# Ring slots between the heads of the first mixer, and the place of the convolutions in the first two parts of each feed-forward

## Chip, cores and metric

The kernel runs on one core of a Trainium2 chip. The metric is the device time of one execution, in microseconds (us). The core has five engines with queues of their own: TensorE (PE in the profile; its weight loads are PEld), VectorE (DVE), ScalarE (ACT), GpSimd (POOL) and SyncE (SP), which here only issues loads and stores. They wait for each other through semaphores. Before the change three runs took 1823.7, 1823.83 and 1827.47 us, with a median of 1823.83.

## What is computed

A two-layer encoder for 256 prompt tokens and 512 sample tokens of width 1024. Each layer has a mixer and a feed-forward, both with adaptive norms (adaln: shifts, scales and gates that are computed from a condition). The mixer of layer 0 is a two-way mLSTM with four heads; that of layer 1 is windowed attention. All is float32. The parts that the change touches, cut to their core:

```python
# mLSTM, per head and direction
s = einsum('bhtd,bhsd->bhts', qc, kc) * exp(log_d - m_t[..., None])
num = einsum('bhts,bhse->bhte', s, vc) + ...
h = num / maximum(abs(den), exp(-m_t)[..., None])
...
hs = h_fwd + h_bwd
hs = hs * rsqrt(mean(hs * hs, axis=-1, keepdims=True) + EPS) * head_g
out = (hs * sigmoid(o)) @ w_out
...
# feed-forward of width 2816: a convolution of width 3 along the tokens behind the first product
u = conv(h @ w_up)          # two halves, a and b
out = (silu(a) * b) @ w_down
```

## The kernel before

**Products.** A float32 product is made of three products of a narrower format: each operand is split into a high and a low part, and high x high, high x low and low x high are summed in PSUM. The split of a weight is a copy on ScalarE (L272, `whi`) and a subtraction on VectorE (L273, `wlo`); `fp_copy_split` does both. So each 128x1024 block of weights costs one load on SP's queue (`raw`, L281, five buffers), one ScalarE and one VectorE instruction, and then runs on TensorE.

**Slabs.** Large intermediate tensors (q, k and v of a head, the broadcast maxima, the transposed result, the rows of the feed-forward) come from one ring of six slots (`slab`). A slot is given in the order of the requests, and a tensor waits for all readers of the tensor that had the slot before. `hsT`, two slabs that take the transposed results of heads 0 and 1 and of heads 2 and 3, is requested ahead of the loop over the heads, but each is first written when a head closes.

**Order.** A list scheduler fixes the order of instructions on each engine from the program, from the estimated ends of what they wait for, and from explicit constraints (`issue_after`: not before that instruction). On the chip each engine then runs its queue strictly in that order.

**The heads.** The loop over four heads: request `mb` (the slab of this head's maxima, and later of its result), load the two rows of maxima, broadcast to 128 partitions (`maxima`, L751; head 0 loads them later, in `values`), compute q and k (`gemmT` and `keep`, evacuated by L275 and L276), scores with the decays (`E`, from L813 to L823), v, and scores times v for each block of 128 tokens (L866 to L874), with the sums of squares for the norm in `ss` (L878, L879). `close` scales a finished sequence on ScalarE (L732), transposes it on TensorE (L736), and writes it to `hsT` (L740); the close of one head is called inside the next. The adaln products of later norms (`ps<-raw,silc`) fill gaps.

**The feed-forward.** The width of 2816 is cut into eleven parts. `up(p)` computes two pairs of 128-column chunks: i = 0 is the half a, i = 1 the half b. For p of 1 and more `pair` uses a scheme with seven products per pair instead of eight; GpSimd prepares sums of the weights (L1381 to L1393), ScalarE copies a PSUM bank to another twice (L1397 and L1408, the `fork`), so that a sum already made can go on in two ways, and VectorE adds at the end (L1421, L1422). Part 0 is computed by a function of its own, with an order written by hand. Then `conv` runs for each chunk: one ScalarE instruction (L1585) and two on VectorE (L1587, L1588), the outer taps. `silu` (L1595) is on ScalarE, which has to load another function table first; `product` (L1600) multiplies on GpSimd and splits the result `g`, which `down(p)` multiplies by the weights of the second product. What is in the list `held` is run inside the next `pair`, behind its second copy. Before the change `held` holds the silu of the first half for p of 1 and more, and for part 0 the silu and product, which so come in the first pair of part 1.

## Time and profile before

| | |
|---|---|
| median of three runs | 1823.83 us |
| profiled execution | 1823.31 us |
| its span | 1821.4 us |
| VectorE, L273 of weights | 231 times, 1378 ns each, 318.2 us |
| GpSimd, L1600 | 44 times, 1966 ns each, 86.4 us |
| loads of 512 KB of `in_w_dram` | 208, 3.7 us from issue to landing |
| loads of 512 KB of `in_adaln_w_dram` by SP into `raw` | 84, 4.5 us from issue to landing |

The program has two layers one after the other, and in each a mixer and then a feed-forward: the passage from head 0 to head 1 lies between about 115 and 190 us, the first feed-forward starts at about 530 us, the second at about 1300 us. A row of a timeline gives the start in us, the duration, the engine, the line and operation, the tensors out<-in, the shapes, how many such instructions were put together, and in brackets the idle time of the engine before it and what ended that. A row of waits gives engine, tensor and line, what it waited for, then the us in total, the number of waits and the longest. Matmuls are pipelined: the time from one start to the next is the pace, and the duration in a row is longer.

### The profile page before, as it was taken

What the parts mean: (1) busy time and instruction counts of PE and PEld (TensorE: products, weight loads), DVE (VectorE), ACT (ScalarE), POOL (GpSimd) and SP (SyncE); (2) the same over time, 40 slices, a digit from 0 to 9 for tenths busy, and PEclk for the clock granted to TensorE, in tenths of its full rate; (3) what the DMA queues carried; (4) which work ended last, traced back from release to release, by engine and by line L of the source; (5) the groups of instructions that cost most, each with busy time, mean ns of one, the idle gap of its engine ahead of it and who ended that gap; (6) DMA issues with size and microseconds to landing.
All of it is one profiled execution on the core that took longest, in us unless ns stands there. A gap on an engine that the chain in (4) does not pass through costs nothing.

```text
span 1821.4 us, 28979 instructions
## 1 busy us (share of the span) xinstructions
PE 1785.9 (98%) x11290; PEld 1652.4 (91%) x11290; DVE 1390.6 (76%) x2148; ACT 891.4 (49%) x1798; POOL 474.1 (26%) x384
## 2 busy tenths in 40 slices
PE   7999999999999999999999999999999999999998
PEld 4987888889998999999999999889989999999997
DVE  4875677786799777787877867767998777787776
ACT  3553433444455444444444556665564444444443
POOL 2100000031024333333331313330144333333321
PEclk9999999999999999999999999999999999999998
DMA  8334456556212222222222331134122222222212
GB/s 337 122 121 139 158 196 221 190 159 222 95 55 73 69 70 69 64 66 70 70 70 86 113 93 42 56 94 138 47 81 70 70 70 70 70 71 70 70 36 70
DMA packets 64245, 184.48 MB, mean 101 GB/s; under 512 B 6167, under 2 KB 23831, under 8 KB 64108
## 3 DMA queue, kind: packets, MB, share of 16 engines
q1 hardware_dynamic: 63532, 182.11, 31.0%
q8 instruction: 89, 1.46, 0.3%
q10 hardware_dynamic: 576, 0.52, 0.1%
q14 instruction: 48, 0.39, 0.1%
HBM read 176.17 MB, written 6.43 MB: 100 GB/s over the span
## 4 chain that ended last, share of the span: by engine, by line
PE 87%; DVE 5%; ACT 3%; DMA 3%; issue 1%; POOL 1%; SPq 0%; POOLq 0%; DVEq 0%; ACTq 0%
PE ps L266 28%; PE pa L266 24%; PE ps L1348 10%; PE ps L1351 10%; PE ps L1349 10%; DMA raw<-in_w_dram 1%; PE pa L1187 1%; DMA raw<-in_adaln_w_dram 1%; DVE wlo L273 1%; ACT whi L272 1%; DMA slab<-in_adaln_w_dram 0%; PE pa L1349 0%; PE pa L1348 0%; DVE wlo L1473 0%; DVE ada L528 0%
## 5 line engine op out<-in xcount | busy, mean ns | idle before, releaser
L273 DVE TENSOR_TENSOR wlo<-raw,whi 128x1024 fp32r<-128x1024 f32 x231 | 318.2, 1378 | 113.0 <-ACT whi L272 111.1
L272 ACT CAST whi<-raw 128x1024 fp32r<-128x1024 f32 x231 | 241.9, 1049 | 331.9 <-PE pa L266 142.5
L266 PE MATMUL pa<-slab,whi 128*128 128x256 f32 (+1 forms) x1328 | 317.8, 334 | 0.0
L266 PEld LDWEIGHTS pa<-slab,whi 128*128 128x128 f32 x1328 | 230.1, 189 | 21.5 <-DVE slab L606 0.2
L606 DVE SCALAR_TENSOR_TENSOR slab<-pa,mod,slab 128x256 f32<-128x256 f32 (+1 forms) x332 | 192.7, 598 | 63.1 <-PE pa L266 63.0
L266 PE MATMUL pa<-slab,wlo 128*128 128x256 f32 (+1 forms) x664 | 213.0, 333 | 0.0
L266 PE MATMUL ps<-zh,whi 128*128 128x256 f32 (+1 forms) x560 | 187.9, 337 | 0.3 <-ACT zh L946 0.3
L266 PE MATMUL ps<-zl,whi 128*128 128x256 f32 (+1 forms) x560 | 184.1, 331 | 0.5 <-DVE zl L574 0.5
L266 PE MATMUL ps<-zh,wlo 128*128 128x256 f32 (+1 forms) x560 | 180.9, 329 | 0.0
L1348 PE MATMUL ps<-zh,whi 128*128 128x384 f32 x504 | 172.5, 342 | 3.8 <-ACT nt L1419 1.9
L1349 PE MATMUL ps<-zl,whi 128*128 128x384 f32 x504 | 170.1, 337 | 0.8 <-DVE zl L1305 0.8
L1351 PE MATMUL ps<-zh,wlo 128*128 128x384 f32 x504 | 169.2, 336 | 0.0
L266 PE MATMUL ps<-slab,whi 128*128 128x384 f32 (+2 forms) x656 | 163.7, 333 | 0.9 <-DVE slab L273 0.5
L266 PEld LDWEIGHTS pa<-slab,wlo 128*128 128x128 f32 x664 | 125.2, 189 | 13.2 <-DVE wlo L273 0.4
L1384 POOL TENSOR_TENSOR raw<-raw,raw 128x512 f32<-128x512 f32 x40 | 53.8, 1346 | 318.6 <-DVE wlo L273 245.7
L1600 POOL TENSOR_TENSOR slab<-slab 128x772 f32<-128x772 f32 x44 | 86.4, 1966 | 171.1 <-DVE slab L1588 159.2
L1587 DVE SCALAR_TENSOR_TENSOR slab<-slab,cstt,slab 128x771 f32<-128x771 f32 x88 | 108.4, 1233 | 26.6 <-ACT slab L1585 26.4
L528 DVE SCALAR_TENSOR_TENSOR ada<-raw,silc,ada 128x1024 f32<-128x1024 f32 x84 | 109.5, 1333 | 12.8 <-DMA raw<-in_adaln_w_dram 12.8
L266 PEld LDWEIGHTS ps<-zl,whi 128*128 128x128 f32 x560 | 106.3, 190 | 13.3 <-issue 4.2
L266 PEld LDWEIGHTS ps<-zh,whi 128*128 128x128 f32 x560 | 106.4, 190 | 13.2 <-issue 4.3
L266 PEld LDWEIGHTS ps<-slab,whi 128*128 128x128 f32 x656 | 115.3, 188 | 3.4 <-ACT whi L272 0.9
L266 PEld LDWEIGHTS ps<-zh,wlo 128*128 128x128 f32 x560 | 105.2, 190 | 9.1
(304 smaller groups left out, 4302.8 us busy)
## 6 DMA issues: line engine op xcount, KB each, us to landing
raw<-in_w_dram SPq DMA_DIRECT2D x208, 512.0 KB, 3.7
raw<-in_adaln_w_dram SPq DMA_DIRECT2D x84, 512.0 KB, 4.5
slab<-in_x_dram SPq DMA_DIRECT2D x12, 512.0 KB, 7.5
slab<-in_adaln_w_dram SPq DMA_DIRECT2D x12, 512.0 KB, 10.3
slab<-mrows SPq DMA_DIRECT2D x8, 384.0 KB, 4.6
xs<-slab SPq DMA_DIRECT2D x6, 512.0 KB, 3.8
bt<-brow SPq DMA_DIRECT2D x16, 192.0 KB, 3.1
slab<-xs SPq DMA_DIRECT2D x6, 512.0 KB, 7.2
```

Source lines behind the costliest of these rows:

```text
L266: self.nc.tensor.matmul(out, lhsT, rhs, start=start, stop=stop)
L272: nc.scalar.copy(hi, src)
L273: return nc.vector.tensor_tensor(lo, src, hi.bitcast(F32), ALU.subtract)
L528: stt(acc[:, s], row, w, acc[:, s], ALU.mult, ALU.add)
L606: self.nc.vector.scalar_tensor_tensor(x, o, self.mod[l][:, gc + c, q : q + 1], x, ALU.mult, ALU.add)
L1187: nc.tensor.transpose(pp[:, ks], b.t[:, e, ks], self.ident)
L1348: mm(o, wh[:, k], hi[k], start=start and k == 0, stop=False, skip_group_check=True)
L1349: mm(o, wh[:, k], lo[k], start=False, stop=False, skip_group_check=True)
L1351: mm(o, wl[:, k], hi[k], start=False, stop=k == 3, skip_group_check=True)
L1384: tt(q[0], q[2], q[0], ALU.subtract)
L1587: stt(y[:, 1:], u[:, :-1], w(0), y[:, 1:], ALU.mult, ALU.add)
L1600: nc.gpsimd.tensor_tensor(y, y, yrow[:, j], ALU.mult)
```

## The change

Two parts, in one diff.

In the mLSTM, `maxima` becomes a function of the head and its slab. The slab of the next head's maxima (`soon`) is requested and loaded in the body of the head before, ahead of the loop over the tokens, and at heads 0 and 2 a GpSimd memset writes one column of the `hsT` slab that this and the next head fill. Both move the moment at which a slot of the ring is taken.

In the feed-forward, `taps(urow, yrow, p, i)` names the two convolutions of a half. Part 0 runs those of its half a at once; those of its half b go to the first pair of part 1 behind its second copy, and its silu and product to the second pair, at the same place. Part 1 runs its convolutions, silu and product after both of its pairs. From part 2 on nothing changes, but the constraint on held work now names the low half of a weight split (`wb_low`) too.

```diff
     def split(self, src):
...
-        self.fp_copy_split(hi, lo, src)
+        self.low = self.fp_copy_split(hi, lo, src)
         return hi, lo
...
+        def maxima(h, mb):
+            for d in range(2):
+                r = d * 32 + h
+                nc.sync.dma_start(mb[:, d], md[r : r + 1, :].to_broadcast([P, T]))
...
         for h in range(4):
 
-            mb = self.slab([P, 4, T])
-
-            def maxima():
...
-            if h:
-                maxima()
+            if h == 0:
+                mb = self.slab([P, 4, T])
+            else:
+                mb = soon
...
+            if h < 3:
+                soon = self.slab([P, 4, T])
+                maxima(h + 1, soon)
+            if h % 2 == 0:
+                nc.gpsimd.memset(hsT[h // 2][:, 0, 0:1], 0.0)
             ss = pool.tile([P, T6], F32, tag="ss", name=self.nm("ss"), bufs=2)
...
         wb = self.split(rb)
+        wb_low = self.low
...
         if behind:
-            with self.tc.issue_after(fork.ins):
+            with self.tc.issue_after(fork.ins), self.tc.issue_after(wb_low.ins):
                 behind()
...
+        def taps(urow, yrow, p, i):
+            for j in range(2):
+                conv(urow[:, 2 * i + j], yrow[:, 2 * i + j], i * FC + 2 * p + j)
...
-                for j in range(2):
-                    conv(urow[:, 2 * i + j], yrow[:, 2 * i + j], i * FC + 2 * p + j)
-                if i == 0:
-                    held.append(lambda: silu(yrow))
-            if p:
-                product(yrow, g)
-            else:
-                gate = held.pop()
-                held.append(lambda: (gate(), product(yrow, g)))
+                if p > 1:
+                    taps(urow, yrow, p, i)
+                    if i == 0:
+                        held.append(lambda: silu(yrow))
+            if p == 0:
+                taps(urow, yrow, 0, 0)
+                held.extend((lambda: (silu(yrow), product(yrow, g)), lambda: taps(urow, yrow, 0, 1)))
+                return g
+            if p == 1:
+                for i in range(2):
+                    taps(urow, yrow, 1, i)
+                silu(yrow)
+            product(yrow, g)
             return g
```

The order of SP's queue around the maxima of heads 0, 1 and 2 (slab_677, slab_1300 and slab_2168 are their slabs), before:

```order
L715 DMA mrows<-slab_294 36x768
L751 DMA slab_677<-mrows 128x768 x2
L281 DMA raw_1462<-in_adaln_w_dram 128x1024
L281 DMA raw_1464<-in_adaln_w_dram 128x1024
L281 DMA raw_1467<-in_w_dram 128x1024
L281 DMA raw_1500<-in_adaln_w_dram 128x1024
L281 DMA raw_1531<-in_w_dram 128x1024
L281 DMA raw_1564<-in_adaln_w_dram 128x1024
L281 DMA raw_1595<-in_adaln_w_dram 128x1024
L751 DMA slab_1300<-mrows 128x768 x2
L751 DMA slab_2168<-mrows 128x768 x2
L281 DMA raw_1625<-in_adaln_w_dram 128x1024
```

And with the change (slab_677, slab_1135 and slab_1965):

```order
L715 DMA mrows<-slab_294 36x768
L732 DMA slab_677<-mrows 128x768 x2
L732 DMA slab_1135<-mrows 128x768 x2
L281 DMA raw_1463<-in_adaln_w_dram 128x1024
L281 DMA raw_1465<-in_adaln_w_dram 128x1024
L281 DMA raw_1468<-in_w_dram 128x1024
L281 DMA raw_1501<-in_adaln_w_dram 128x1024
L281 DMA raw_1532<-in_w_dram 128x1024
L281 DMA raw_1565<-in_adaln_w_dram 128x1024
L281 DMA raw_1596<-in_adaln_w_dram 128x1024
L732 DMA slab_1965<-mrows 128x768 x2
L281 DMA raw_1626<-in_adaln_w_dram 128x1024
```

Head 1's maxima moved ahead of seven weight loads, right behind head 0's; head 2's stayed where they were.

VectorE at the close of head 0, where the low half of head 1's q (slab_1303) is written from four PSUM tiles (L276), before:

```order
L740 TENSOR_SCALAR slab_675<-pa_1286,cstt 128x512
L872 TENSOR_SCALAR slab_677<-pa_1271,dn_1262,slab_677 128x256
L740 TENSOR_SCALAR slab_675<-pa_1292,cstt 128x512
L276 TENSOR_SCALAR slab_1303<-ps_1310,slab_1303 128x512
L276 TENSOR_SCALAR slab_1303<-ps_1351,slab_1303 128x256
L276 TENSOR_SCALAR slab_1303<-ps_1388,slab_1303 128x512
L276 TENSOR_SCALAR slab_1303<-ps_1419,slab_1303 128x256
L878 TENSOR_SCALAR ss_1135<-ss_1135 128x2
```

With the change the first two of the four stand far ahead of the close (which writes slab_675 in L745, 36 rows below the last row shown here), among the scores of head 0:

```order
L273 TENSOR_TENSOR PT_1060<-E_1051,PT_1059 128x640
L276 TENSOR_SCALAR slab_1304<-ps_1311,slab_1304 128x512
L724 COPY eT<-pa_1127 128x216
L813 TENSOR_SCALAR E_1088<-slab_677,aT,kct 128x128
L273 TENSOR_TENSOR PT_1078<-E_1070,PT_1077 128x640
L813 TENSOR_SCALAR E_1088<-slab_677,aT,kct 128x128
L813 TENSOR_SCALAR E_1110<-slab_677,aT,kct 128x128 x2
L273 TENSOR_TENSOR wlo_1535<-raw_1532,whi_1534 128x1024
L276 TENSOR_SCALAR slab_1304<-ps_1352,slab_1304 128x256
```

The block of four behind the first writes of `hsT` is taken apart.

ScalarE in the first feed-forward, around the silu of part 0 (slab_5576; L1408 is the second copy of the first pair of part 1), before:

```order
L1585 ACTIVATE slab_5576<-slab_5126,cstt 128x772
L1408 COPY ps_4555<-ps_4554 128x384
L1595 ACT_TABLE_LOAD
L1595 ACTIVATE slab_5576<-slab_5576 128x772
L272 COPY whi_5708<-raw_5698 128x1024
L1361 COPY slab_5126<-pa_5398 128x128
L1361 COPY slab_5126<-pa_5398 128x256
L272 COPY slab_5577<-slab_5576 128x772
L1585 ACTIVATE slab_5576<-slab_5126,cstt 128x772
L1595 ACTIVATE slab_5576<-slab_5576 128x772
```

And with the change (L1414 is now the second copy, here of the second pair; L1601 the silu; slab_5578 part 0; slab_5579 its product, slab_5586 part 1):

```order
L1414 COPY ps_4557<-ps_4556 128x384
L1601 ACT_TABLE_LOAD
L1601 ACTIVATE slab_5578<-slab_5578 128x772 x2
L272 COPY s1h_6082<-raw_6071 128x512
L1425 COPY nt_5753<-ps_4557 128x384
L1408 COPY nt_5982<-ps_4555 128x384
L272 COPY slab_5579<-slab_5578 128x772
L1591 ACTIVATE slab_5586<-slab_5129,cstt 128x772 x2
L272 COPY whi_5875<-raw_5873 128x1024
L272 COPY slab_5579<-slab_5578 128x772
L1591 ACTIVATE slab_5586<-slab_5129,cstt 128x772
```

The table load, the silu and the casts of part 0's product moved from the first pair of part 1 to behind the second copy of the second; part 1's convolutions (L1591) stand between the two casts.

More of the change, by code (lines that the diff above doesn't have):

```diff
@@ L744, in mlstm @@
         for h in range(4):
-            mb = self.slab([P, 4, T])
-            def maxima():
-                for d in range(2):
-                    r = d * 32 + h
-                    nc.sync.dma_start(mb[:, d], md[r : r + 1, :].to_broadcast([P, T]))
-            if h:
-                maxima()
+            if h == 0:
+                mb = self.slab([P, 4, T])
+            else:
+                mb = soon
             qk = []
@@ L786, in evac @@
                         self.step(self.fillp)
-                self.gemmN(U_MIN + 3 * h + 2, evac, None if h else (decay, maxima))
+                self.gemmN(U_MIN + 3 * h + 2, evac, None if h else (decay, lambda: maxima(0, mb)))
                 return v
```

## The prediction

> **What bounds the kernel now.** I read the page's busy shares first, then the waits of TensorE by stretch, then the order of time around the places where TensorE stands still.

> ```profile
> span 1821.4 us, 28979 instructions
> ...
> PE 1785.9 (98%) x11290; PEld 1652.4 (91%) x11290; DVE 1390.6 (76%) x2148; ACT 891.4 (49%) x1798; POOL 474.1 (26%) x384
> ```

> TensorE is busy for 1785.9 of 1821.4 us, so no edit can win more than 35.5 us by removing idle time, plus what a low clock costs inside busy time. The profiled execution took 1823.31 us, 1.9 more than its span, and the median of the runs is 1823.83, 0.5 above it. The waits of TensorE from 125 to 190 us (heads 0 and 1 of the first layer) come first, those from 540 to 580 us (the start of the first feed-forward) second; from 1305 to 1350 us (the second feed-forward) the three largest rows read the same.

> ```profile
> PE ps L266 <- DVE slab L276: 2.4, 1, 2.4
> PE pa L266 <- ACT slab L272: 1.5, 1, 1.5
> PE pa L736 <- ACT slab L732: 0.8, 1, 0.8
> ```

> ```profile
> PE ps L1351 <- DVE s1l L273: 1.4, 1, 1.4
> PE ps L1348 <- ACT nt L1419: 1.0, 1, 1.0
> PE ps L1348 <- ACT ps L1397: 0.7, 1, 0.7
> ```

> These two places are the ones that the change edits. The windows (TensorE, weight load, VectorE, ScalarE, GpSimd busy, then the granted clock) show what else happens there.

> ```profile
> 140.00:145.00 5.00, 5.00 (x34) 2.52 (x27) 2.09 (x8) 1.88 (x5) 0.72 (x1) 0.50 0.00 0
> ```

> ```profile
> 560.00:565.00 5.00, 3.63 (x21) 3.26 (x20) 5.00 (x5) 4.28 (x8) 3.37 (x2) 1.00 0.34 105
> ```

> After the stall in the heads the clock is granted at 0.50; in the feed-forward it stays at 1.00, and VectorE is busy without a break.

> **The heads: ring slots in order of need.** The rows of TensorE, with those of the engines that it waits for:

> ```profile
> 135.76 1.63 PE L736 MATMUL pa<-kct,slab 128*128 128x128 f32 x8 [0.75 <-ACT slab L732]
> 139.77 3.63 PE L266 MATMUL ps<-raw,silc 128*32 128x256 f32 x30 [2.38 <-DVE slab L276]
> 143.33 0.80 PE L266 MATMUL ps<-zh,whi 128*128 128x512 f32 x1
> ...
> 145.47 0.39 PE L266 MATMUL ps<-zh,wlo 128*128 128x512 f32 x1
> 145.70 0.40 PE L266 MATMUL ps<-zh,whi 128*128 128x512 f32 x1
> ...
> 146.86 0.38 PE L736 MATMUL pa<-kct,slab 128*128 128x128 f32 x2
> 146.99 0.48 PE L266 MATMUL ps<-zh,wlo 128*128 128x512 f32 x1
> ```

> ```profile
> 181.51 1.07 PE L266 MATMUL ps<-raw,silc 128*32 128x256 f32 x16
> 184.08 0.51 PE L266 MATMUL pa<-slab,PT 128*128 128x258 f32 x2 [1.50 <-ACT slab L272]
> ```

> ```profile
> 137.32 0.75 DVE L740 TENSOR_SCALAR slab<-pa,cstt 128x512 f32<-128x512 f32 x1 [1.61 <-PE pa L736]
> ...
> 139.03 1.94 DVE L276 SCALAR_TENSOR_TENSOR slab<-ps,slab 128x512 fp32r<-128x512 f32 x4
> ```

> ```profile
> 182.42 1.04 ACT L272 CAST whi<-raw 128x1024 fp32r<-128x1024 f32 x1 [1.62 <-DMA raw<-in_w_dram]
> ...
> 183.67 0.35 ACT L272 CAST slab<-ps 128x256 fp32r<-128x256 f32 x1
> ```

> The evacuations of head 1's q (L275, L276) run as one block of four behind head 0's close (L740), because q's slot comes after that of hsT in the ring. Their four PSUM tiles stay full until 139.03 and later, and the adaln matmuls have no bank. In the changed order the same eight instructions stand one by one between the score and value work of head 0, each behind the product that it evacuates, and the transposes of L736 stand between the products of head 1's k. So these stalls go:
> - the wait of 0.75 ahead of the transposes;
> - their pace: eight take 1.63, while a pair later takes 0.13 (146.86 to 146.99), four pairs 0.5: 1.1;
> - the wait of 2.38 for a bank;
> - the low clock after it. Thirty adaln matmuls take 3.56 us (139.77 to 143.33) where sixteen at full clock take 1.07, thirty then 2.0: 1.6. The five products from 143.33 to 145.47 take 2.14 where one a 0.23 (145.47 to 145.70) makes 1.15: 1.0. Together 2.6;
> - the wait of 1.50 at 184: the copy of v (183.67) stands behind a weight copy that waits for its load (182.42). In the new order two more v products (48 matmuls of 128x256) stand between that v product and its reader; at half of 0.23 each these are 5.5 us of cover for 1.5.

> Sum: 0.75 + 1.1 + 2.4 + 2.6 + 1.5 = 8.3 us. What is added: one GpSimd memset of 128x1 at heads 0 and 2, on an engine that is 26% busy; and the two loads of head 1's maxima, moved ahead of three weight loads.

> ```profile
> 127.20 21.59 SPq L751 DMA_DIRECT2D slab<-mrows  x4
> ```

> ```profile
> SPq L751 <- PE pa L736: 19.6, 1, 19.6
> ```

> ```profile
> slab<-mrows SPq DMA_DIRECT2D x8, 384.0 KB, 4.6
> ```

> The four maxima loads hold SP for 21.59 us, of which 19.6 wait for the last transposes of head 0; two adaln loads and head 1's v weights are queued behind. The change takes only two of the four out; head 2's still wait for the close at the same place. So the block ends no later than before, by as much earlier as the close is, and the v weights have the cover that they had. The two moved loads (4.6 us to landing) delay weights that are read only some 30 us later. I put both at zero. The bounds of this part: 4.2 if the waits go but a stall elsewhere still takes the clock down and the wait at 184 stays (0.75 + 1.1 + 2.4), 8.3 if nothing comes instead. All four heads are ordered anew, and TensorE hardly waits in the other three, so a little can only be lost there; I take 7.5.

> [...]

> **The feed-forward: work behind the copies.** Both layers have the same new order. VectorE's work stays the same; only its place changes. Prices:

> ```profile
> 547.57 1.28 ACT L1595 ACT_TABLE_LOAD   x1
> 548.86 0.85 ACT L1595 ACTIVATE slab<-slab 128x772 f32<-128x772 f32 x1
> ...
> 552.33 0.84 ACT L272 CAST slab<-slab 128x772 fp32r<-128x772 f32 x1 [1.24 <-POOL slab L1600]
> 553.07 1.03 ACT L1585 ACTIVATE slab<-slab,cstt 128x772 f32<-128x772 f32 x1
> ...
> 558.73 0.48 ACT L1397 COPY ps<-slab 128x384 f32<-128x384 f32 x1 [2.59 <-DVE slab L1421]
> ```

> ```profile
> 547.82 1.21 DVE L273 TENSOR_TENSOR wlo<-raw,whi 128x1024 fp32r<-128x1024 f32 x1
> ...
> 561.15 2.14 DVE L273 TENSOR_TENSOR s1l<-raw,s1h 128x512 fp32r<-128x512 f32 x1
> ...
> 566.38 1.01 DVE L1588 SCALAR_TENSOR_TENSOR slab<-slab,cstt,slab 128x771 f32<-128x771 f32 x1
> 567.31 0.95 DVE L273 TENSOR_TENSOR slab<-slab,slab 128x772 fp32r<-128x772 f32 x1
> ```

> ```profile
> 549.79 2.51 POOL L1600 TENSOR_TENSOR slab<-slab 128x772 f32<-128x772 f32 x1 [5.97 <-ACT slab L1595]
> ...
> 560.90 1.84 POOL L1600 TENSOR_TENSOR slab<-slab 128x772 f32<-128x772 f32 x1 [4.43 <-DVE slab L1588]
> ```

> ```profile
> 561.63 0.34 PE L1349 MATMUL ps<-zl,s1h 128*128 128x384 f32 x1
> 563.35 0.44 PE L1351 MATMUL ps<-zh,s1l 128*128 128x384 f32 x1 [1.37 <-DVE s1l L273]
> ```

> Removed: the three waits, 1.4 + 1.0 + 0.7 = 3.1; and each costs a little more than its row says: 561.63 to 563.35 is 1.72, and the pace of 128x384 is 0.17 (three quarters of the 0.23), so the third costs 1.55 where its row has 1.37. With the same 0.17 on each, 3.6 a layer. s1l and the copies no longer stand behind part 0's silu and product.

> Added: the silu and products of part 0 come behind the second copy of pair two, and down(0), which needs them, directly behind that pair. Three waits can take the place:
> - the first pair's sums (L1422) still stand behind the taps: 0 to 1.0, I take 0.3.
> - the second copy of pair two now has no product between its input and its reader. TensorE waits for the copy, 0.48, and its signals: 0.7.
> - down(0). From the end of that copy TensorE has three products of twelve, 36 x 0.17 = 6.2 us. Table load 1.28, silu 0.85, GpSimd 1.84 to 2.51, cast 0.84: the first high half is there after 4.8 to 5.5, in time; its low half, 0.95 more, too. The second half is later: ScalarE puts two conv starts of part 1 (2 x 1.03) and a weight copy (1.04) ahead of its cast, ready at 8.7 to 9.4. VectorE, idle before, then has three taps, a weight low half, a tap and the product's low half: 4 x 1.01 + 1.21 + 0.95 = 6.2 from about 6.4, ready at 12.6 (12 to 13.5). TensorE has used up its 6.2 and twelve products of 0.23, then four more, by 9.9, waits 0.9 for a weight copy, and stands again from 11.2: 1.4, bounds 0.8 to 2.3. Small waits behind it 0.3. In all 2.6, bounds 1.9 to 3.5.

> Sum 0.3 + 0.7 + 2.6 = 3.6, bounds 2.6 to 5.2: nothing gained or lost against the 3.6 removed, from -1.0 to +1.6 a layer. I take 0 for both layers, bounds -2.0 to +3.2.

> Forecast: 1823.3 - 7.5 + 0 = 1815.8 by the profiled execution, 0.5 more by the median: **1816**.

> **Rivals.**
> 1. The heads' gain is partly given back. For: SP still waits 19.6 us for the close; head 1's v weights now sit behind reads of the adaln weights that come a little later. A load (4.6 as that of the maxima), copy 1.04 and low half 1.21 make 6.9, against 24 score products of 0.23, 12 half as wide and nine thin adaln ones, 7 to 8 us. If that cover fails and the clock falls again, only the 4.2 stay: 1819.6, or half a us more.
> 2. The feed-forward gains in full. For: VectorE has the same work with fewer clashes with GpSimd (s1l at 2.14). Against: the chain above. Without new waits 2 x 3.6 more: 1809.
> 3. Slower: the clock. If the stand ahead of down(0) reaches the 2.4 us that brought 0.50 at 140, each layer pays 2.6 for the clock besides the upper bound of its waits: (5.2 - 3.6 + 2.6) x 2 = 8.4, more than the 7.5 of the heads; with the heads at their 4.2 it ends at 1823.8 - 4.2 + 8.4 = 1828. It decides from a stand of 2.4 us; mine is 1.4. Against: 560 to 565 holds stands of 1.4 at clock 1.00.
> 4. The change does not do it: the slots still come late. The new order speaks against it; 1823.8.

> **How the numbers follow.** Forecast 0.62, rival 1 0.14, rival 2 0.10, rival 3 0.11, rival 4 0.03. A change under 0.2%, 3.6 us, can't be told from none: faster is below 1820.2. The forecast and rival 2 lie there, and of rival 1 about a third: 0.77. Rival 4 and the rest of rival 1: 0.12. Rival 3: 0.11. The likeliest case's own range is 1813 to 1819.5 (8.3 and -2.0 to 7.5 and +3.2); the range of 1809 to 1824 takes in the first two rivals and leaves out the third.

> **What would show it.** Right: no wait of L276 and no window of clock under 0.9 between 125 and 190, TensorE busy there for all but about 1 us; behind the second copy of pair two (near 555 in a span that is shorter) a wait of 0.7 and, at down(0), one or two of 1 to 2 us on L273. Wrong: a new TensorE wait over 1 us between 125 and 400, a clock of 0.5 in the feed-forward, or a feed-forward that loses less than 2 or more than 5 us a layer.

## The result, and the profile after

The changed kernel is slightly slower: its median is 1827.14 us (1824.25 to 1831.24, nine runs) where the kernel before has 1823.73 (1823.44 to 1827.47, nine runs). The ratio is 1.0020, with a 95% interval of 1.0011 to 1.0029. The forecast was 1816 within 1809 to 1824, so both the size and the direction were wrong. The profiled execution took 1831.24 us, the longest of the nine; before's took 1823.31.

The top of the page of the changed kernel, span and busy time of each engine:

```profile
span 1829.4 us, 28977 instructions
...
PE 1791.7 (98%) x11290; PEld 1654.3 (90%) x11290; DVE 1383.3 (76%) x2148; ACT 889.5 (49%) x1798; POOL 474.6 (26%) x386
```

TensorE has the same 11290 instructions as before and is busy for 5.8 us longer, so the first question is where the clock fell. These are windows of the changed kernel (busy time of TensorE, weight load, VectorE, ScalarE, GpSimd, then the granted clock): the place of the old stall in the heads first, then the start of down(0) in both layers.

```profile
140.00:145.00 5.00, 5.00 (x35) 4.46 (x34) 1.43 (x7) 2.13 (x8) 0.69 (x1) 1.00 0.01 2
...
575.00:580.00 5.00, 3.87 (x10) 3.10 (x11) 5.00 (x7) 1.00 (x2) 1.73 (x1) 0.66 0.33 105
1360.00:1365.00 5.00, 3.19 (x8) 2.58 (x9) 5.00 (x6) 1.67 (x2) 1.05 (x1) 0.66 0.36 105
```

The last two stretches before:

```profile
575.00:580.00 5.00, 5.00 (x34) 4.72 (x33) 5.00 (x6) 2.52 (x4) 1.52 (x2) 1.00 0.34 105
1360.00:1365.00 5.00, 5.00 (x34) 4.81 (x33) 5.00 (x7) 1.59 (x3) 4.63 (x3) 1.00 0.08 34
```

The clock of 0.50 between the heads is gone, as forecast; a new low clock stands in each feed-forward, where it was 1.00. The waits of TensorE in the feed-forward of the first layer (540 to 600 us) show what comes ahead of it:

```profile
PE pa L266 <- DVE slab L273: 2.4, 1, 2.4
PE ps L1353 <- ACT ps L1414: 0.6, 1, 0.6
PE ps L1353 <- DVE slab L1428: 0.4, 1, 0.4
```

The three waits of before (1.4, 1.0, 0.7) are gone. Of those that came instead, 0.37 for the sums and 0.61 for the second copy are what the prediction had (0.3 and 0.7), but the stand ahead of down(0) is 2.40 where 1.4 was forecast. TensorE's rows there:

```profile
573.39 0.34 PE L1354 MATMUL ps<-yl,whi 128*128 128x384 f32 x1
576.13 0.65 PE L266 MATMUL pa<-slab,whi 128*128 128x512 f32 x1 [2.40 <-DVE slab L273]
576.58 0.63 PE L266 MATMUL pa<-slab,wlo 128*128 128x512 f32 x1
...
579.14 0.63 PE L266 MATMUL pa<-slab,wlo 128*128 128x512 f32 x1
579.57 0.42 PE L1356 MATMUL ps<-yh,wlo 128*128 128x384 f32 x1
```

Eight products take 3.44 us (576.13 to 579.57), 0.43 each. VectorE's rows show what the product of part 0 was waiting behind (L1593 and L1594 are the sums of the convolutions; the two `slab<-slab,slab` of L273 are the low halves of the product):

```profile
559.59 1.23 DVE L273 TENSOR_TENSOR wlo<-raw,whi 128x1024 fp32r<-128x1024 f32 x1 [0.40 <-ACT whi L272]
566.12 1.21 DVE L273 TENSOR_TENSOR s1l<-raw,s1h 128x512 fp32r<-128x512 f32 x1 [5.30 <-ACT s1h L272]
567.25 0.54 DVE L1428 TENSOR_TENSOR slab<-pa,nt 128x384 f32<-128x384 f32 x1
567.72 2.15 DVE L273 TENSOR_TENSOR slab<-slab,slab 128x772 fp32r<-128x772 f32 x1
569.80 0.55 DVE L1427 TENSOR_TENSOR slab<-ps,nt 128x384 f32<-128x384 f32 x1
570.26 1.94 DVE L1593 SCALAR_TENSOR_TENSOR slab<-slab,cstt,slab 128x771 f32<-128x771 f32 x2
...
574.19 1.01 DVE L1594 SCALAR_TENSOR_TENSOR slab<-slab,cstt,slab 128x771 f32<-128x771 f32 x1
575.12 0.95 DVE L273 TENSOR_TENSOR slab<-slab,slab 128x772 fp32r<-128x772 f32 x1
```

VectorE, which worked here without a break before, stands idle for 5.30 us at 560.8 to 566.1; then the sums of part 1 come ahead of the product's second low half, which TensorE needs and which ends at 576.07.

In the heads the picture is the other way round. The waits of TensorE from 100 to 400 us:

```profile
PE ps L266 <- DMA raw<-in_adaln_w_dram: 1.7, 1, 1.7
PE pa L266 <- DVE E L823: 1.2, 2, 0.7
PE ps L266 <- ACT whi L272: 0.6, 1, 0.6
PE ps L266 <- DVE wlo L273: 0.6, 2, 0.3
PE ps L491 <- DVE sb L487: 0.4, 1, 0.4
```

None of the three waits of before (2.4, 1.5, 0.8) is left, and SP still stands 19.2 us for head 2's maxima, both as forecast. But there are five new rows. To see their effect I match each TensorE instruction with the same one of the profile before and take the median difference of the starts, the *shift*. It is -5.4 at 150 to 160 and still -5.1 at 200 to 230, then -3.7 at 270 to 290, -1.7 at 310 to 340 and 0.0 from 350 on. The heads win about 5 us and have lost them again 120 us later. The first feed-forward adds 2.5; the second takes the shift from 2.8 to 6.2. Of these 3.4, 0.9 comes ahead of the first pair, with a wait of 0.84 for `zl` that stands with 0.94 to 0.96 in e1, e8 and e10 below too, two of which have the old feed-forward; the other 2.5 are those of the first layer again. The span grows by 8.0; the last 1.6 of it come behind 1800 us, and e4 below, whose shift is 0.0 up to there, has 1.7 there too.

### The profile page after: what moved, and what is told of

Its sections match the earlier page's. It is cut to its first block, busy times and chain, and to the rows that moved or that the text cites. A ratio compares the mean times of both kernels' runs of the same rounds, so it can differ in the third digit from the quotient of the medians.

```text
span 1829.4 us, 28977 instructions
## 1 busy us (share of the span) xinstructions
PE 1791.7 (98%) x11290; PEld 1654.3 (90%) x11290; DVE 1383.3 (76%) x2148; ACT 889.5 (49%) x1798; POOL 474.6 (26%) x386
## 4 chain that ended last, share of the span: by engine, by line
PE 82%; DVE 7%; DMA 4%; ACT 4%; issue 2%; POOL 0%; SPq 0%; POOLq 0%; DVEq 0%; ACTq 0%
PE ps L266 24%; PE pa L266 23%; PE ps L1353 11%; PE ps L1356 10%; PE ps L1354 10%; DMA raw<-in_w_dram 2%; DMA raw<-in_adaln_w_dram 2%; PE pa L1192 1%; ACT whi L272 1%; DVE ada L528 1%; DVE wlo L273 1%; PE pa L1354 1%; PE pa L1353 1%; PE pa L1356 1%; DMA slab<-in_adaln_w_dram 0%
## 5 line engine op out<-in xcount | busy, mean ns | idle before, releaser
L272 ACT CAST whi<-raw 128x1024 fp32r<-128x1024 f32 x231 | 241.8, 1049 | 361.1 <-PE pa L266 154.8
L273 DVE TENSOR_TENSOR wlo<-raw,whi 128x1024 fp32r<-128x1024 f32 x231 | 309.0, 1339 | 115.8 <-ACT whi L272 113.8
L266 PE MATMUL pa<-slab,whi 128*128 128x256 f32 (+1 forms) x1328 | 319.6, 335 | 4.8 <-DVE slab L273 4.8
L266 PEld LDWEIGHTS pa<-slab,whi 128*128 128x128 f32 x1328 | 231.3, 189 | 27.6 <-DVE slab L273 5.8
L606 DVE SCALAR_TENSOR_TENSOR slab<-pa,mod,slab 128x256 f32<-128x256 f32 (+1 forms) x332 | 193.2, 598 | 72.1 <-PE pa L266 72.0
L266 PE MATMUL pa<-slab,wlo 128*128 128x256 f32 (+1 forms) x664 | 214.3, 335 | 0.0
L266 PE MATMUL ps<-zh,whi 128*128 128x256 f32 (+1 forms) x560 | 187.6, 336 | 0.9 <-ACT whi L272 0.6
L266 PE MATMUL ps<-zl,whi 128*128 128x256 f32 (+1 forms) x560 | 183.4, 330 | 0.5 <-DVE zl L574 0.5
L266 PE MATMUL ps<-zh,wlo 128*128 128x256 f32 (+1 forms) x560 | 180.5, 328 | 0.6 <-DVE wlo L273 0.6
L266 PE MATMUL ps<-slab,whi 128*128 128x384 f32 (+2 forms) x656 | 163.7, 332 | 0.9 <-DVE slab L273 0.5
L266 PEld LDWEIGHTS pa<-slab,wlo 128*128 128x128 f32 x664 | 126.3, 190 | 13.1
L1593 DVE SCALAR_TENSOR_TENSOR slab<-slab,cstt,slab 128x771 f32<-128x771 f32 x88 | 112.2, 1279 | 25.7 <-ACT slab L1591 25.6
L266 PEld LDWEIGHTS ps<-zh,whi 128*128 128x128 f32 x560 | 106.1, 190 | 13.9 <-issue 3.9
L266 PEld LDWEIGHTS ps<-slab,whi 128*128 128x128 f32 x656 | 115.2, 188 | 3.4 <-ACT whi L272 0.9
L266 PEld LDWEIGHTS ps<-zl,whi 128*128 128x128 f32 x560 | 106.0, 190 | 12.2 <-issue 3.4
L266 PEld LDWEIGHTS ps<-zh,wlo 128*128 128x128 f32 x560 | 104.9, 189 | 10.1 <-DVE wlo L273 1.0
## 6 DMA issues: line engine op xcount, KB each, us to landing
slab<-mrows SPq DMA_DIRECT2D x8, 384.0 KB, 4.7
```

What stands on the lines that cost most here:

```text
L266: self.nc.tensor.matmul(out, lhsT, rhs, start=start, stop=stop)
L272: nc.scalar.copy(hi, src)
L273: return nc.vector.tensor_tensor(lo, src, hi.bitcast(F32), ALU.subtract)
L606: self.nc.vector.scalar_tensor_tensor(x, o, self.mod[l][:, gc + c, q : q + 1], x, ALU.mult, ALU.add)
L1593: stt(y[:, 1:], u[:, :-1], w(0), y[:, 1:], ALU.mult, ALU.add)
```

## The experiments

Two theories were tried. The first: the heads' half of the change is worth nothing in the end, since its gain is given back by new waits in heads 2 and 3, and the feed-forward half is the whole loss, by the stand ahead of down(0) and its clock. The rival: heads 2 and 3 are limited by the stream of weights anyhow, and the rest is spread between runs. That spread is large enough to matter: over the later runs the kernel before had medians of 1824.46 to 1825.94 with single runs between 1820.1 and 1831.5. Each kernel is compared below with the runs of before beside it, and shifts are against the one profile of before.

| kernel | what it holds of the change | median us | before beside it | ratio, 95% interval |
|---|---|---|---|---|
| e1_heads | heads half | 1823.79 | 1824.81 | 0.9996 (0.9987 to 1.0005) |
| e2_ffn | feed-forward half | 1829.51 | 1824.81 | 1.0030 (1.0019 to 1.0042) |
| e3_heads_first | head 1's maxima, head 0's memset | 1822.38 | 1824.81 | 0.9987 (0.9978 to 0.9996) |
| e4_ffn_p0now | only part 1 deferred | 1825.12 | 1824.81 | 1.0003 (0.9992 to 1.0013) |
| e5_ffn_low | feed-forward half, product's low half first | 1833.52 | 1824.46 | 1.0050 (1.0034 to 1.0067) |
| e6_best | e5 and e3 | 1829.25 | 1824.46 | 1.0026 (1.0016 to 1.0035) |
| e7_first_mem2 | e3 and head 2's memset | 1825.81 (one run) | 1824.46 | |
| e8_mem0 | head 0's memset alone | 1821.96 (one run) | 1824.46 | |
| e9_fill | feed-forward half, part 1's first taps not deferred | 1824.93 | 1824.65 | 1.0000 (0.9991 to 1.0010) |
| e10_fill_mem0 | e9 and e8 | 1820.51 | 1824.65 | 0.9976 (0.9967 to 0.9985) |
| e11_mem0_5 | e8 again, timed | 1819.86 | 1824.65 | 0.9978 (0.9968 to 0.9989) |
| e12_both_mem | memsets of heads 0 and 2 alone | 1820.57 | 1825.94 | 0.9978 (0.9967 to 0.9990) |

### The two halves apart

**e1_heads** takes the edits of the mixer alone; the feed-forward is that of the kernel before.

```diff
+            if h < 3:
+                soon = self.slab([P, 4, T])
+                maxima(h + 1, soon)
+            if h % 2 == 0:
+                nc.gpsimd.memset(hsT[h // 2][:, 0, 0:1], 0.0)
```

> Only the heads' half of the change. Theory (the heads win about 5.3 us up to 230 us and lose as much again by new waits in heads 2 and 3; the whole loss is the feed-forward's): 1822.5 to 1824.5, TensorE 5 us early at 230 us and not early at 360, the runs within about 1 us of each other as before, no clock under 0.9 between 100 and 1790 us. Rival (the new order of the heads is what costs): 1826 to 1828.

**e2_ffn** takes the other half, `wb_low` too; the mixer is that of the kernel before.

```diff
+            if p == 0:
+                taps(urow, yrow, 0, 0)
+                held.extend((lambda: (silu(yrow), product(yrow, g)), lambda: taps(urow, yrow, 0, 1)))
+                return g
+            if p == 1:
+                for i in range(2):
+                    taps(urow, yrow, 1, i)
+                silu(yrow)
```

> Only the feed-forward's half. Theory (the stand of 2.4 us ahead of down(0) brings the clock down in some executions and not in others): 1825 to 1831 with runs several us apart, one window of clock near 0.66 behind each stand. Rival (the waits were 3.1 a layer and are 3.4, so the edit is nearly neutral): 1823.5 to 1824.5, runs within 1 us.

The heads half comes out at 0.9996 and the feed-forward half at 1.0030; their product, 1.0026, is the changed kernel within the intervals. So the loss is the feed-forward's, and the heads' forecast gain does not reach the end.

The feed-forward half alone has the same stand in both layers, 2.39 us each time. Its windows there:

```profile
575.00:580.00 5.00, 3.13 (x14) 2.49 (x15) 5.00 (x7) 1.75 (x2) 0.98 (x1) 1.00 0.36 105
1360.00:1365.00 5.00, 4.92 (x16) 4.24 (x17) 5.00 (x7) 0.04 (x1) 2.69 (x2) 0.66 0.22 83
```

The clock fell in the second layer but not in the first. TensorE's rows of both, in the same execution:

```profile
576.87 0.50 PE L266 MATMUL pa<-slab,whi 128*128 128x512 f32 x1 [2.39 <-DVE slab L273]
577.21 0.39 PE L266 MATMUL pa<-slab,wlo 128*128 128x512 f32 x1
...
578.94 0.44 PE L1351 MATMUL ps<-yh,wlo 128*128 128x384 f32 x1
```

```profile
1360.08 0.50 PE L266 MATMUL pa<-slab,whi 128*128 128x512 f32 x1 [2.39 <-DVE slab L273]
1360.42 0.44 PE L266 MATMUL pa<-slab,wlo 128*128 128x512 f32 x1
1360.66 0.63 PE L266 MATMUL pa<-slab,whi 128*128 128x512 f32 x1
...
1363.86 0.42 PE L1349 MATMUL ps<-yl,whi 128*128 128x384 f32 x1
1364.12 0.34 PE L1351 MATMUL ps<-yh,wlo 128*128 128x384 f32 x1
```

Without the low clock the eight products take 2.07 us (576.87 to 578.94), in the changed kernel with it 3.44: the low clock costs 1.4. The layers agree: the first adds 1.3 to the shift (0.7 to 2.0), the second 2.6 (2.0 to 4.6). A stand of 2.4 us thus costs about 1.3 a layer more than the waits it replaced, and 1.3 again where the clock falls, which it did at three of the four such stands in these two profiles.

The record of the granted clock shows what sets the fourth apart. In every trace the moments at which the clock changes lie whole multiples of 3.41 us apart. In e2 it fell at 1360.62; counted back in such steps, one lies at 575.55. It cuts the first layer's stand (574.48 to 576.87) into 1.1 and 1.3 us. The second layer's stand (1357.69 to 1360.08) lies whole inside one step, 1357.21 to 1360.62. In the changed kernel the clock fell at 576.32 and 1361.39, and TensorE was idle for 2.5 and 2.1 us of the step ahead of each.

### The feed-forward: where the stand comes from

The edits of e4, e5 and e9 are shown against e2.

**e4_ffn_p0now** leaves part 0 as before and defers part 1 alone.

```diff
             if p == 0:
-                taps(urow, yrow, 0, 0)
-                held.extend((lambda: (silu(yrow), product(yrow, g)), lambda: taps(urow, yrow, 0, 1)))
+                taps(urow, yrow, 0, 0)
+                taps(urow, yrow, 0, 1)
+                held.append(lambda: (silu(yrow), product(yrow, g)))
                 return g
```

> Of the feed-forward's half only the deferral of part 1's convolutions: part 0's are run at once and its silu and product come in the first pair of part 1, as before the change. Theory (part 0's product behind the second pair makes the stand; VectorE's queue made the old waits): no stand over 1 us ahead of down(0), the old waits of 3.1 a layer at most half left, 1818 to 1822, runs within 1 us. Rival (the order of part 1's convolutions makes the stand): as slow as the whole half, 1825 or more.

1.0003, so nothing of it came. The trace says why: TensorE's waits are those of before (0.99, 0.72 and 1.35 us), and its shift in the feed-forward stays within 0.1. Deferring part 1 alone left the order of VectorE's rows from 550 to 580 as it was, so its theory, that this would take the old waits away, fell. What removes the old waits is the move of part 0, and part 1 matters only with it.

**e5_ffn_low** takes the stand away by force: part 1's sums are ordered behind the product's last low half.

```diff
-                self.fp_copy_split(g[:, 0, j], g[:, 1, j], y)
+                self.done = self.fp_copy_split(g[:, 0, j], g[:, 1, j], y)
...
             if p == 1:
-                for i in range(2):
-                    taps(urow, yrow, 1, i)
-                silu(yrow)
+                with self.tc.issue_after(self.done.ins):
+                    for i in range(2):
+                        taps(urow, yrow, 1, i)
+                    silu(yrow)
```

> The feed-forward half of the change alone, with one order added: part 1's four convolutions and its silu are emitted behind the last low half of part 0's product, so that in VectorE's order that low half (0.95 us) stands ahead of the three convolution sums of part 1 (1.94 and 1.01 us in one row pair, then 1.01) that stand in front of it in the changed kernel. Theory (the loss is the stand ahead of down(0), made by those sums in VectorE's queue, and the clock that falls behind it): the wait of 2.39 to 2.40 us for L273 ahead of down(0) falls to at most 0.3 us in both layers, the granted clock in 575 to 580 and 1360 to 1365 stays at 1.00, the waits removed by the change (0.97, 0.71 and 1.37 us a layer before) stay small, and TensorE's shift over a layer turns from +1.3 to +2.8 us to about -1 us: 1821 to 1823 where before is 1824.8, 6 to 8 us under the half without this order. Rival A (the work is only late elsewhere): the wait comes back in front of down(1) or of the next pair, and the time stays within 2 us of the half alone, 1828 to 1831. Rival B (clock only, not the stand): waits fall but the clock still falls in the same stretch; 1825 to 1827.

The theory as put there fell, and its rival A held in kind, with a loss beyond its 1828 to 1831: 1.0050, more than the half alone. The wait for the product is gone and the clock from 575 to 580 and 1360 to 1365 stays at 1.00, but the wait comes back in pieces. TensorE's waits from 575 to 620 us:

```profile
PE ps L1351 <- DVE wlo L273: 3.1, 3, 1.4
PE ps L1348 <- ACT ps L1398: 0.9, 1, 0.9
PE pa L266 <- DVE slab L606: 0.4, 1, 0.4
```

The first layer adds 3.4 to the shift and the second 5.0. In the second the clock falls after all, only later, behind waits of 0.88 and 0.75 (0.50 from 1400.56 to 1403.97), which fits the 1.6 between the layers:

```profile
1400.00:1404.00 4.00, 4.00 (x16) 4.00 (x15) 2.07 (x3) 1.84 (x3) 0.00 (x0) 0.57 0.64 178
```

VectorE has no idle time from 580 to 600 us there: whatever comes first, something else that TensorE needs comes last. Pushing work back further made it worse.

**e6_best** joins this with the heads edit of e3 (below).

> The run before joined with head 1's early maxima and the memset of head 0 alone (heads 2 and 3 as before). If the two act in stages that do not touch each other, their gains add: heads -2.4 (median of that part alone against before) to -4 us (its trace), feed-forward -2 to -3 us, so 1818 to 1821 where before is 1824.8, and TensorE's shift is about -4 to -5 from 250 on, about -5 after the first feed-forward and -6 after the second. Rival (the heads' gain is taken back by weight loads that come no earlier, so that the feed-forward begins when it did): the shift returns to 0 by 540 and the time is that of the run before, 1821 to 1823.

It lost for the same reason: 3.4 and 4.9 us in the feed-forwards, with a low clock from 1389.72 in the second again, against -5.4 from the heads, 1.0026.

**e9_fill** goes the other way and puts work back into VectorE's hole: part 1's first taps run when their rows are there, as before the change, and only its silu is held, behind the second high half of part 0's product on ScalarE (`self.done` is that cast here).

```diff
-                if p > 1:
+                if p:
                     taps(urow, yrow, p, i)
-                    if i == 0:
+                    if i == 0 and p > 1:
                         held.append(lambda: silu(yrow))
...
             if p == 1:
-                for i in range(2):
-                    taps(urow, yrow, 1, i)
-                silu(yrow)
+                with self.tc.issue_after(self.done.ins):
+                    silu(yrow)
```

> The feed-forward half with part 0 as in the change, but part 1's first two convolutions run as soon as their rows are there, as before the change, and only its silu is held, behind the second high half of part 0's product on ScalarE. In the changed kernel VectorE stood idle for 5.30 us at 560.8 to 566.1, because part 1's sums had all been put behind both pairs, and then had them in front of the product's low half. Theory (the loss is work taken out of that hole and put in front of the product): four sums of 1.01 us go back into the hole, the wait of 2.40 us ahead of down(0) falls to at most 0.5 us, the clock at 575 to 580 and 1360 to 1365 stays at 1.00, and the waits of 0.36 and 0.61 us stay: shift of -0.5 to -1.5 us a layer, 1821.5 to 1823.5 where before is 1824.5. Rival (VectorE has no room there, the work of both parts simply does not fit ahead of down(0)): waits of 1 us and more for wlo or slab (L273) in 570 to 615 as in the run that put the low half first (1.38, 1.03, 0.87, 0.73), shift +1 to +4 a layer, 1827 to 1833.

The windows of this kernel show the hole filled (VectorE, the third number behind the length, had 4.70 of the ten us from 560 in the changed kernel) and the clock whole:

```profile
560.00:570.00 10.00, 9.45 (x55) 9.13 (x54) 9.15 (x9) 9.50 (x15) 4.90 (x3) 1.00 0.33 106
570.00:575.00 5.00, 4.96 (x24) 3.93 (x23) 4.97 (x5) 4.50 (x6) 1.21 (x1) 1.00 0.08 12
575.00:580.00 5.00, 5.00 (x31) 4.65 (x30) 5.00 (x6) 2.36 (x5) 3.18 (x2) 1.00 0.26 96
580.00:590.00 10.00, 8.14 (x46) 7.01 (x45) 10.00 (x11) 4.13 (x6) 5.66 (x4) 1.00 0.00 0
```

The stand of 2.40 is gone, and with it the whole loss: 1.0000. Each layer adds only 0.2 to the shift. But no gain came either (-0.5 to -1.5 a layer was expected), though the waits of before are gone. TensorE's waits from 550 to 620 us name the next one:

```profile
PE pa L266 <- DVE slab L606: 1.9, 2, 1.1
PE ps L1348 <- ACT ps L1409: 0.6, 1, 0.6
PE ps L1348 <- DVE slab L1423: 0.4, 1, 0.4
```

L606 adds down(0) to the residual on VectorE and frees the banks; it now stands behind a sum of 1.98 us and a low half of 2.49 (TensorE's waits are 1.06 and 0.80 at 585 and 588). So the 3.1 us of waits that were removed come back as 2.9 here, as 3.4 in the changed kernel and as 5.4 in e5: VectorE is busy for 29.1 of the 30 us from 560 to 590, and these orders only choose which of its results TensorE waits for. Of the 29.1, 7.0 are what six rows take beyond their usual length, each of them beside a GpSimd instruction (1.93, 1.48, 2.16, 2.57, 1.98 and 2.49, where the same forms take 1.01, 0.68, 0.95, 1.01, 1.01 and 0.95). No run moved GpSimd's products, so whether room could be made there is not tested.

### The heads: which edit wins, which loses

**e3_heads_first** keeps head 1's early maxima and head 0's memset, and leaves heads 2 and 3 as before; its edit is shown against e1.

```diff
-            if h < 3:
+            if h == 0:
                 soon = self.slab([P, 4, T])
-                maxima(h + 1, soon)
-            if h % 2 == 0:
+                maxima(1, soon)
+            if h == 0:
                 nc.gpsimd.memset(hsT[h // 2][:, 0, 0:1], 0.0)
```

> Of the heads' half only what concerns heads 0 and 1: head 1's maxima early, the memset at head 0 alone; the later slabs and loads as before the change. Theory (the give-back comes from the early slab of head 3 and the memset at head 2): the 5.3 us stay, 1818 to 1819.5. Rival (heads 2 and 3 are held by the loads whatever the order, and give back what comes early): 1823 to 1824.

Its median lies between theory and rival: 1822.38, 2.4 below that of before, while the trace keeps a shift of -3.6 to -4.0 from 250 to 1790 us.

**e7_first_mem2** adds head 2's memset to e3.

```diff
-            if h == 0:
+            if h % 2 == 0:
                 nc.gpsimd.memset(hsT[h // 2][:, 0, 0:1], 0.0)
```

> Heads alone: head 1's maxima early and both memsets (heads 0 and 2), but the maxima of heads 2 and 3 where they were. In the whole heads half the shift of TensorE went from -5.4 at 200 to 230 to -0.9 at 330; with head 1's maxima and head 0's memset alone it went from -5.2 to -3.9 and stayed. Theory: the early maxima of heads 2 and 3 take the ring's slots ahead of what these heads need next, and make the new waits at 301 to 304 (0.40, 0.62 and 0.30 us): without them the shift stays at -3.5 to -4.5 from 250 to 1800. Rival: head 2's memset takes its slot of the ring too early: the shift goes back to -1 by 330, with the same waits. One look of a kernel whose runs differ by some 3 us, so the trace's shifts decide, not the time: 1818 to 1823 by the theory, 1822 to 1825 by the rival.

**e8_mem0** is the kernel before with two lines more.

```diff
                 for c in range(2):
                     self.ahead(U_MIN + (3 * h + 3, 12)[h == 3], c)
+            if h == 0:
+                nc.gpsimd.memset(hsT[h // 2][:, 0, 0:1], 0.0)
```

> Heads alone: nothing but the GpSimd memset of one column of head 0's slab (its slot of the ring is taken ahead of the loop over the tokens instead of at the first write); all maxima where they were. Theory (both parts are needed: the memset orders the writes behind the slot, the maxima give head 1 its operands): the shift at 200 to 230 is under half of the 5.2 us, 0 to -2.5, and the low clock at 140 to 145 (0.50 before) is still there. Rival (the slot alone does it): shift -5 at 200 to 230, clock 1.00 through 110 to 150. By the trace's shifts, one look: 1819 to 1825.

**e11_mem0_5** is the same kernel again, with nine runs.

> The memset of head 0's slab alone again, timed. Theory (this one edit is the whole gain of the heads half, -6.2 us at 200 to 230 and -4.9 kept to 1200 in the first look): 1819.5 to 1822 where before is 1824.5, ratio 0.997 to 0.9985. Rival (the look was one of the lower runs of a kernel that is no faster): 1823 to 1825, ratio within 0.999 to 1.001.

**e12_both_mem** has both memsets and nothing else, against the kernel before.

```diff
+            if h % 2 == 0:
+                nc.gpsimd.memset(hsT[h // 2][:, 0, 0:1], 0.0)
```

> Both memsets of the change (heads 0 and 2) and nothing else; all maxima where they were. It differs from the run that gained 4.8 us in the median by head 2's memset alone. Theory (head 2's memset takes its slot of the ring ahead of what heads 2 and 3 need, and gives the gain back): the waits of 0.40, 0.62 and 0.30 us (L491, whi, wlo) at 300 to 304 are there, TensorE's shift goes from about -6 at 200 to 230 to -1 to -3 by 340, and the median lies 2 to 4 us above that run's: 1822 to 1824. Rival (the early maxima of heads 2 and 3 are needed for the loss too): no such waits, the shift stays at -5, 1819 to 1821.

TensorE's shift, by what a kernel has of the heads' edits:

| edits in the heads | kernels | at 80 to 95 us | at 200 to 220 us | at 400 us |
|---|---|---|---|---|
| none | e2, e4, e5, e9 | 0.0, -0.9, +0.3, -0.2 | -0.4, -1.8, -1.1, -1.6 | +0.7, +0.1, +5.3, +1.9 |
| head 0's memset | e8, e10, e11 | +0.2, -0.6, -0.6 | -6.2, -6.9, -7.0 | -4.9, -5.6, -5.4 |
| both memsets | e12 | +0.1 | -6.3 | -3.4 |
| head 0's memset, head 1's maxima | e3, e6 | 0.0, -0.2 | -5.2, -5.3 | -4.0, -5.4 |
| the same and head 2's memset | e7 | +0.2 | -5.0 | +0.3 |
| all | e1, the change | -0.8, +0.3 | -5.4, -5.1 | -1.1, 0.0 |

The first row is the caution: without any edit in the heads the shift at 400 moves between +0.1 and +5.3 from one execution to the next, in e5 with one wait of 2.19 for an adaln load at 358 (e7's +0.3 holds one of 1.80 at 355). A single shift of 2 us proves nothing. I go by waits that stand in every trace with an edit and in none without it. The shift at 80 to 95 us, ahead of every edit in the heads, is spread between executions too. Counted from there, the shift at 200 to 220 is -6.3 to -6.4 in all four traces with head 0's memset and without the early maxima, -4.7 to -5.4 in the five with them, and -0.4 to -1.4 with no edit: in the one profile of before the low clock in the heads lasted 6.83 us, as in e2, and in e4, e5 and e9 only 3.41.

*The gain is the memset of head 0 alone.* My theory for e8, that the maxima are needed too, fell, and the rival held: -6.2 at 200, clock 1.00 at 140 to 145. Timed, it is 0.9978, 4.8 us in the median. Its window where the clock had been 0.50:

```profile
140.00:145.00 5.00, 5.00 (x37) 4.60 (x36) 2.99 (x9) 2.48 (x6) 0.70 (x1) 1.00 0.00 2
```

The first write of `hsT` now comes ahead of the loop over the tokens, so the ring gives its slot out early and head 1's q no longer stands behind it: in this kernel's order of VectorE all four rows of L276 for that q stand ahead of the first L740 of head 0. Head 1's maxima then come by themselves at 110.4 instead of 127.2.

*Head 1's early maxima lose about a microsecond* (6.3 to 6.4 against 4.7 to 5.4). They put two loads more on SP ahead of the weights. ScalarE's cast of the weight that is loaded behind them, before and in e3:

```profile
105.93 1.05 ACT L272 CAST whi<-raw 128x1024 fp32r<-128x1024 f32 x1 [2.26 <-DMA raw<-in_w_dram]
```

```profile
108.08 1.05 ACT L272 CAST whi<-raw 128x1024 fp32r<-128x1024 f32 x1 [4.46 <-DMA raw<-in_w_dram]
```

And TensorE, some 9 us later, in e3:

```profile
117.66 0.59 PE L266 MATMUL pa<-slab,PT 128*128 128x258 f32 x3 [0.99 <-DVE E L825]
```

The cast starts at 107.8 to 108.4 in all five traces with these loads (the changed kernel, e1, e3, e6, e7) and at 105.2 to 106.5 in the nine without; the wait for E, 0.7 to 1.4 us, is in all of the first and in none of the second.

*Head 2's memset loses about two.* TensorE's rows of e12, which stand with the same lengths in e1, e7 and the changed kernel and in no other:

```profile
299.04 0.63 PE L491 MATMUL ps<-kct,sb 128*128 128x128 f32 x2 [0.40 <-DVE sb L487]
300.28 0.50 PE L266 MATMUL ps<-zh,whi 128*128 128x512 f32 x1 [0.62 <-ACT whi L272]
301.54 0.50 PE L266 MATMUL ps<-zh,wlo 128*128 128x512 f32 x1 [0.30 <-DVE wlo L273]
```

ScalarE casts this weight at 299.18 in e12 and at 291.81 in e11: with the memset, the close of head 2 comes ahead of it in ScalarE's order. The shift goes from -5.7 at 280 to -3.5 at 310, as it does from -4.0 to -1.9 in e7, whose rival held by this. In the median this does not show: e12 and e11 both have 0.9978, with intervals wide enough for 2 us. The rival for e12, that the early maxima of heads 2 and 3 are needed for these waits, is ruled out, but that e12 would lie 2 to 4 us above e11 did not come true.

**e10_fill_mem0** joins head 0's memset with the filled feed-forward.

> The run before joined with the memset of head 0 alone. If the gains add: heads -4 to -5 in TensorE's shift from 250 to 540, then -0.5 to -1.5 for each feed-forward, so -5 to -8 in the trace at 1780 and 1817 to 1820 in the median where before is 1824.5 (the one look at the memset alone was 1821.96, 2.5 below the median of before). Rival (the heads' gain does not last beyond a run's spread): 1821 to 1824.

0.9976, the same as the memset alone: the feed-forward half adds nothing even in its best form of these. The simplest of the fastest kernels is the kernel before with the one memset: 1819.86 us, 0.9978 of before (0.9968 to 0.9989), which beats both kernels of this case; e10 and e12 can't be told from it.

## Why the prediction was wrong

- **The waits between heads 0 and 1 go, with the low clock after them: right.** All three are gone and the clock is 1.00. The sum of 8.3 was too large: the edit that does it brings 6.3 to 6.4 in the trace. Counted from each start to the next over 100 to 230 us in e11, the products ahead of the transposes gave 0.8 (forecast 0.75), the transposes with the wait behind them 3.3 (1.1 + 2.4), the adaln matmuls with the wait behind them 2.1 (1.6 + 1.5), and all the rest together lost 0.5 where the five products were to give 1.0.
- **Which edit does it: not seen.** The forecast treated maxima and memset as one. The memset of head 0 is the gain; head 1's early maxima and head 2's memset are losses in every trace that has them, and the early maxima of heads 2 and 3 were not run alone.
- **"I put both at zero" for the two moved loads: wrong.** The two loads moved ahead of seven weight loads, not three, and the step looked at the readers some 30 us later and not at the loads issued next. The cast of one of these came 2.2 us later (105.93 to 108.08) and TensorE waited 0.7 to 1.4 us.
- **"A little can only be lost there" in heads 2 and 3: mis-sized.** In place of 0.8 (8.3 to 7.5), head 2's memset alone costs about 2, and with the maxima and one wait of 1.73 for an adaln load nothing is left of the 7.5 at 360. Only the load was in rival 1, at another place; since loads like it also come in kernels with no edit in the heads, I do not count it to the change.
- **SP still held by head 2's maxima; the wait at 184 gone: right** (19.2 us; no such wait).
- **The first pair's sums 0.3, the second copy 0.7: right** (0.37 and 0.61).
- **"Ready at 12.6 (12 to 13.5)" for the product's second low half: the step that decided.** From the end of the copy (562.68) it was ready after 13.4 (576.07), and TensorE stood from 11.05 (forecast 11.2, though its own terms, 9.9 and 0.9, give 10.8). VectorE did the six pieces in the 5.8 us that were priced at 6.2, but began 1.2 late: the product's *first* low half took 2.15 where it was priced at 0.95. GpSimd's products ran beside it:

```profile
564.92 4.13 POOL L1606 TENSOR_TENSOR slab<-slab 128x772 f32<-128x772 f32 x2 [0.87 <-ACT slab L1601]
```

  The slow form was in the profile before: s1l, quoted at 2.14 beside a GpSimd product (L1600, 560.90 to 562.74), against 1.21 for a tile twice as wide. In the trace of the changed kernel the low half of a product takes 0.94 to 0.96 in the 24 cases with no GpSimd instruction beside it, and 1.38 to 2.15 in the 20 with one. This one started at 567.72 and ended 0.8 us after GpSimd's last product did (569.05), near its 0.95 alone; how the one slows the other is not shown.

  Counted as the prediction counts, from start to start less the pace of 0.17, the waits of the changed kernel in the first layer are 0.54 + 0.78 + 0.36 + 2.57 = 4.25 where the sum was 3.6: the stand was 1.2 longer, and the 0.9 for a weight copy was 0.36. With the low clock's 1.4 this makes 2.1 of the 2.5 us a layer where 0 was forecast; the rest is spread over matmuls that became a little slower.
- **Rival 3 at 0.11 was what happened**, with its own point of decision: it was to decide from a stand of 2.4 us, the stand was 2.40, and its 1828 is 0.9 from the median. That nearness is in part luck: its price was not right, 1.4 us for a low clock of 3.41 us, not the 2.6 of the heads, where it had lasted 6.83, and not every time (nor was it the wait of 2.38 alone that brought 0.50 there: the clock fell at 138.44, inside that wait, which began at 137.39); the missing part is that the heads gave back all rather than keeping 4.2.
- **"VectorE's work stays the same; only its place changes": true, and by the traces the reason why nothing was won.** The forecast looked for the wait of the next instruction. Before, VectorE was busy for 48.6 of the 50 us from 540 to 590, and in e9 for 49.1, so work moved from one place there came back at another in every order tried. That no order can win there is argued, not shown.

What stays open: what decides the clock when TensorE is idle for 1.6 to 1.8 us of a step, whether moving GpSimd's products would make room on VectorE, and why the medians of e11 and e12 do not show the 2 us that their traces do.

## What to carry to other kernels

When work is put behind something, look at the engine that does it: here the move left a hole of 5.30 us on VectorE, which was full afterwards (10.00 of the ten us from 570), and the wait only changed its name; filling the hole again was worth more than choosing what comes first. Price a VectorE operation that may run beside GpSimd at its slow form: here the low half of a product took 2.15 us where 0.95 was priced. And when an edit has several parts that "order" the same resource, time the smallest part alone: here one memset of one column was worth more than the whole change.

## What the runs showed of the hardware

With two loads more ahead of it on SP's queue, a weight took 2.2 us longer from issue to cast. In e3 the weight behind head 1's maxima was issued at 101.39 and cast at 108.08, 6.7 us; before, issued at 101.45 and cast at 105.93, 4.5.
